# Causal mask of the attention scores: two products of 64 moving columns, one 64x64 triangle, in place of two of 128 columns

## The chip, the cores and the metric

The kernel runs on one core of one Trainium2 chip. The metric is the device time of one execution in microseconds. Before the change three runs took 2469.01, 2470.95 and 2475.01 us; the median is 2470.95.

## What is computed

One layer of a hybrid decoder block for 2048 positions and a model width of 1024, in float32: a modulated RMSNorm, a combined projection, three groups of heads side by side (mLSTM memory, forgetting attention, a chunked spatial gate), an output projection, and a feed-forward part with a causal convolution. The change lies in the attention, which has 8 heads of 64 and works on blocks of 128 queries:

```
for blk in range(s_len // Q_BLOCK):                 # Q_BLOCK = 128, s_len = 2048
    lo, hi = blk * Q_BLOCK, (blk + 1) * Q_BLOCK
    logits = (einsum('bhtd,bhsd->bhts', q[:, :, lo:hi], k[:, :, :hi]) * scale
              + F[:, :, lo:hi, None] - F[:, :, None, :hi])
    mask = (lo + arange(Q_BLOCK))[:, None] >= arange(hi)[None, :]
    logits = where(mask, logits, -inf)
    p = softmax(logits, axis=-1)
    outs.append(einsum('bhts,bhsd->bhtd', p, v[:, :, :hi]))
```

Only the last 128 keys of a query block, the diagonal block, need the mask: key column j is allowed for query row t when j <= t.

## The kernel before

The program goes through the projection, with the mLSTM and the spatial gate in between (0 to about 645 us), then the attention (to about 1010 us, its first scores beside the end of the projection), the output projection, and the feed-forward part.

In the attention, `score` (L194) makes the scores of one query block of one head against up to 1024 keys. q and k are each split into a high and a low float32r part, so a score is three products (high by high, high by low, low by high). The depth of a head is 64, half of TensorE's 128 rows. So the even key blocks of 128 lie on partitions 0 to 63 (`lower`) and the odd ones on 64 to 127 (`upper`), and each of the three terms is two matmuls, one in each row half, each moving up to four key blocks (512 columns). Both write into one PSUM pair `pr` of two banks, one bank for each half. That is line L218. `own` is the half in which the diagonal block lies; it alternates from one query block to the next.

The mask is added on TensorE as well, in L223, after the three terms and only for the chunk that holds the diagonal (`last`). There are 128 such chunks, 16 query blocks of 8 heads. Only the 64 rows of the own half can be used without touching the other half, and a mask of 128 query rows by 128 keys needs a contraction over 128. So the mask comes in two products over 64 rows each, both with 128 moving columns and a stationary matrix of 64 by 128: `identb` with `maskb` brings one half of the mask's query rows, and `idents` with `masks`, the same two with their halves swapped, brings the other. All are bf16; a masked place gets -1e30.

VectorE then runs L224 on the pair: it subtracts from the log-forget bias `nf`, writes the negated logits `L` to SBUF, and keeps their running minimum `nm`. It is also what makes the pair free for the next use; there are two pairs under the tag `pb` and one under `pc`. `weigh` takes the exponential on ScalarE (L232) and scales on GpSimd (L233, L234); `turn_pair` transposes the weights on TensorE in row halves, 64 moving columns each (L248), and copies them to SBUF (L252 to L255); `value_pair` multiplies with the values in column halves of the array (L266). The order of all these steps is a string written by hand (one letter for each: S for score, X for weigh, T, U or W for turns, V for values, Y or Z to leave), and it is kept as it stands by `tc.manual_schedule()`. So each engine has a fixed order in this stage.

The constants are made at the start of the program: on GpSimd the identity `ident` and a 128x128 triangle `m32` (L424, L425), and on VectorE the bf16 copies (L98, L103, L426, L428). After them VectorE goes on with other small constants and then waits for the first statistics of the norm (L558).

Of the kernel before, what the change touches and what calls it, by code (L numbers as in the profile page):

```python
# [10 lines left out]
BF16 = mybir.dt.bfloat16  # L11
AF = mybir.ActivationFunctionType
ALU = mybir.AluOpType
# [4 lines left out]
P = 128  # L18
# [5 lines left out]
NEG = -1.0e30  # L24
# [9 lines left out]
def trunk(  # L34
# [7 lines left out]
    V, A, G, T = nc.vector, nc.scalar, nc.gpsimd, nc.tensor  # L42
# [15 lines left out]
    cst = ctx.enter_context(tc.tile_pool(name="cst", bufs=1))  # L58
# [20 lines left out]
    ident = cst.tile([P, P], F32, name="ident")  # L79
# [14 lines left out]
    sh2 = cst.tile([P, KT], F32, name="sh2")  # L94
    cs = cst.tile([P, KT], F32, name="cs")
    gq8 = cst.tile([P, 1], F32, name="gq8")
    identb = cst.tile([P, P], BF16, name="identb")
    V.tensor_copy(identb, ident)  # L98
    maskb = cst.tile([P, P], BF16, name="maskb")
    idents = cst.tile([P, P], BF16, name="idents")  # L100
    masks = cst.tile([P, P], BF16, name="masks")
    for n in range(2):
        V.tensor_copy(idents[:, 64 * n : 64 * n + 64], ident[:, 64 - 64 * n : 128 - 64 * n])  # L103

    class Mem:

# [50 lines left out]
    def place(b):  # L157
        return 4 + b // 2 if b % 2 else 3 - b // 2
# [5 lines left out]
    def pair():  # L164
        n_pair[0] += 1
        last = three[0] and n_pair[0] % 3 == 0
        return pp.tile([P, 2, 512], F32, name="pr", tag="pc" if last else "pb")
# [26 lines left out]
    def score(h, tb, i, c):  # L194

        kk, nf = kv[h]
        q2, qs = qs_[h, tb], slice(i * P, (i + 1) * P)
        n_b = tb * 4 + i + 1
        if c == 0:
            tag = {(0, 0): "LX", (0, 1): "L2", (NH - 1, 2): "L1"}.get((h, tb), "L%d" % tb)  # L200
            L_[h, tb, i] = (
                pool.tile([P, n_b * P], F32, name="L", tag=tag),
                pool.tile([P, 2], F32, name="nm", tag="nm"), pool.tile([P, 1], F32, name="rs", tag="rs"),
            )
        L, nm, _ = L_[h, tb, i]
        n_p = min(8, n_b - 8 * c)
        ne, no = (n_p + 1) // 2, n_p // 2
        sp = pair().rearrange("p f n -> p (f n)")
        o, w = (4 - ne) * P, n_p * P
        halves_ = [  # L210
            (r, sp[:, a : a + m * P], slice(c * 512 + k0, c * 512 + k0 + m * P))
            for r, a, m, k0 in ((lower, o, ne, o), (upper, 512, no, 0)) if m
        ]
        last = c == (n_b - 1) // 8
        own = (n_b - 1) % 2
        for n, (a, b) in enumerate(((0, 0), (0, 1), (1, 0))):
            for f, (r, dst, ks) in enumerate(halves_):
                T.matmul(dst, q2[a][r, qs], kk[b][r, ks], start=n == 0, stop=n == 2 and not (last and f == own))  # L218
        if last:
            r = (lower, upper)[own]  # L220
            at = place((n_b - 1) % 8) * P
            for a, b in ((identb, maskb), (idents, masks)):
                T.matmul(sp[:, at : at + P], a[r], b[r], start=False, stop=a is idents)  # L223
        V.tensor_tensor_reduce(  # L224
            out=L[:, c * 1024 : c * 1024 + w], in0=sp[:, o : o + w], in1=nf[:, c * 1024 + o : c * 1024 + o + w],
            scale=-1.0, scalar=3.0e38 if c == 0 else nm[:, 0:1], op0=ALU.add, op1=ALU.min, accum_out=nm[:, c : c + 1],
        )
# [194 lines left out]

    m32 = pool.tile([P, P], F32, name="m32", tag="kw")
    G.memset(m32, 0.0)  # L424
    G.affine_select(m32, m32, pattern=[[-1, P]], compare_op=ALU.is_ge, fill=NEG, base=0, channel_multiplier=1)  # L425
    V.tensor_copy(maskb, m32)  # L426
    for n in range(2):
        V.tensor_copy(masks[64 * n : 64 * n + 64], m32[64 - 64 * n : 128 - 64 * n])  # L428
    V.memset(rmask, 1.0)
    V.memset(rmask.rearrange("p (n l) -> p n l", l=P)[:, :, 0:1], 0.0)  # L430

# [842 lines left out]
    for n, (half, i) in enumerate(steps):  # L1274
# [5 lines left out]
        if n == len(steps) - 1:  # L1280
            while background:
                if next(background[0], True):
                    background.pop(0)
            n_accs[0] = 2
            pool.close("proj_r")
            pp.close("proj_r")
            attention_open_right()

            load_k(0)

            def early(tb):
                for i in range(4):
                    score(0, tb, i, 0)
                    yield
                    weigh(0, tb, i)

            for tb in (1, 0):
                load_q(0, tb, "qA")
            first = [early(1), early(0)]
            load_v(0, (0, 1))  # L1300
            background += first
# [71 lines left out]
    for a in order:  # L1373
        if a == "S":
            x_ = s_list.pop(0)
            h, tb, i, c = x_
            if i == 0 and c == 0:
                n = heads.index((h, tb))
# [3 lines left out]
                if n + 1 == len(heads) or heads[n - 1][0] != h or n == 0:  # L1382
                    if h + 1 < NH and h + 1 not in kv:
                        load_k(h + 1)
                        if h % 2:
                            load_v((h + 1) // 2, range(4))
            score(*x_)
            if c == (tb * 4 + i) // 8:
                x_list.append((h, tb, i))
# [563 lines left out]
    at = lambda i, what: getattr(groups[steps[i][1], steps[i][2]], what)(steps[i][3])  # L1953
# [183 lines left out]
```

## Time and profile before

| what | value |
| --- | --- |
| median of three runs | 2470.95 us |
| profiled execution, its own time | 2468.99 us |
| its span, first to last instruction | 2467.0 us |
| granted TensorE clock, mean | 0.998 |
| TensorE products, busy | 2436.6 us (99%) |
| TensorE weight loads, busy | 1973.8 us (80%) |
| VectorE, busy | 1876.9 us (76%) |
| ScalarE, busy | 1198.9 us (49%) |
| GpSimd, busy | 378.7 us (15%) |
| attention stage | 645 to 1010 us of the span |

PE stands for TensorE's products and PEld for its weight loads, DVE for VectorE, ACT for ScalarE, POOL for GpSimd, SP for the queue that issues the DMAs. A row of a group gives line, engine, operation, tiles, shape and count, then the busy time in us, the mean duration of one in ns, and the idle time of the engine ahead of it with what ended it. A row of a timeline gives the start, the duration to the last end, engine, line, tiles, shape and the count of instructions merged in it. A row of waits gives who waited for whom, the total in us, the number of times and the longest. A row of a window gives its length, then for each engine busy time and count, then the granted clock, the share of the DMA engines and GB/s. A shape such as 64*128 64x512 is the part of the array in use (rows by columns) and the operand (partitions by elements). Matmuls are pipelined: the records of several overlap, and the busy time of a line is the time that its records cover.

### The profile page before, as it was taken

What the parts mean: (1) busy time and instruction counts of PE and PEld (TensorE: products, weight loads), DVE (VectorE), ACT (ScalarE), POOL (GpSimd) and SP (SyncE); (2) the same over time, 40 slices, a digit from 0 to 9 for tenths busy, and PEclk for the clock granted to TensorE, in tenths of its full rate; (3) what the DMA queues carried; (4) which work ended last, traced back from release to release, by engine and by line L of the source; (5) the groups of instructions that cost most, each with busy time, mean ns of one, the idle gap of its engine ahead of it and who ended that gap; (6) DMA issues with size and microseconds to landing.
All of it is one profiled execution on the core that took longest, in us unless ns stands there. A gap on an engine that the chain in (4) does not pass through costs nothing.

```text
span 2467.0 us, 39340 instructions
## 1 busy us (share of the span) xinstructions
PE 2436.6 (99%) x14553; PEld 1973.8 (80%) x14553; DVE 1876.9 (76%) x3170; ACT 1198.9 (49%) x2068; POOL 378.7 (15%) x417
## 2 busy tenths in 40 slices
PE   7999999999999999999999999999999999999999
PEld 6888888888766666788778888888888888888887
DVE  6657746476277777756798888879888878988897
ACT  5443343433367777544555444445444445444443
POOL 2023310133257665200000000000000000000000
PEclk9999999999999999999999999999999999999999
DMA  8345753545555453677332222283222229387523
GB/s 272 109 145 160 229 168 90 153 137 167 158 172 150 122 166 106 209 265 269 116 97 91 86 78 86 82 311 94 77 86 86 86 102 326 114 287 239 174 73 119
DMA packets 288823, 373.50 MB, mean 151 GB/s; under 512 B 31102, under 2 KB 181596, under 8 KB 287608
## 3 DMA queue, kind: packets, MB, share of 16 engines
q1 hardware_dynamic: 288632, 371.00, 47.6%
q8 instruction: 114, 1.87, 0.3%
q14 instruction: 77, 0.63, 0.1%
HBM read 274.34 MB, written 96.58 MB: 150 GB/s over the span
## 4 chain that ended last, share of the span: by engine, by line
PE 50%; DVE 1%; ACT 0%; issue 0%
PE ub L55 11%; PE ub L56 11%; PE ub L54 11%; PE db L56 6%; PE db L54 6%; PE db L55 6%; DVE T L1545 0%; DVE hz L1536 0%; DVE wspl L1601 0%; DVE B L1545 0%; ACT hz L1514 0%; ACT T L1541 0%; DVE s L1640 0%; DVE S L1587 0%; DVE u L1634 0%
## 5 line engine op out<-in xcount | busy, mean ns | idle before, releaser
L54 PE MATMUL acc<-wh,hh 128*128 128x512 f32 (+2 forms) x752 | 278.6, 371 | 0.0
L54 PE MATMUL ub<-T,wsph 128*128 128x512 f32 x704 | 273.9, 389 | 1.2 <-ACT wsph L1597 1.2
L55 PE MATMUL ub<-T,wsph 128*128 128x512 f32 x704 | 274.4, 390 | 0.5 <-DVE T L1545 0.5
L56 PE MATMUL ub<-T,wspl 128*128 128x512 f32 x704 | 273.9, 389 | 0.0
L56 PE MATMUL acc<-wh,hl 128*128 128x512 f32 (+2 forms) x752 | 269.6, 360 | 0.3 <-DVE hl L586 0.2
L55 PE MATMUL acc<-wl,hh 128*128 128x512 f32 (+2 forms) x752 | 268.7, 359 | 0.6 <-DVE wl L628 0.6
L55 PE MATMUL db<-wspl,wsph 128*128 128x512 f32 x616 | 239.5, 389 | 0.0
L54 PE MATMUL db<-wsph 128*128 128x512 f32 x616 | 239.5, 389 | 0.0
L56 PE MATMUL db<-wsph,wspl 128*128 128x512 f32 x616 | 239.5, 389 | 0.0
L1597 ACT CAST wsph<-S 128x512 fp32r<-128x512 f32 x176 | 109.3, 622 | 218.1 <-PE ub L55 154.4
L1740 ACT CAST wsph<-act 128x512 fp32r<-128x512 f32 x154 | 96.1, 624 | 230.1 <-PE db L55 221.5
L55 PE MATMUL ub<-B,wsph 128*128 128x512 f32 x528 | 205.6, 389 | 1.0 <-DVE B L1545 0.9
L54 PE MATMUL ub<-B,wsph 128*128 128x512 f32 x528 | 205.7, 390 | 0.0
L56 PE MATMUL ub<-B,wspl 128*128 128x512 f32 x528 | 205.4, 389 | 0.0
L224 DVE CUSTOM_DVE_ANT_0 L<-pr,nf 128x1024 f32<-128x1024 f32 (+7 forms) x128 | 124.3, 989 | 64.4 <-PE pr L218 31.1
L232 ACT ACTIVATE L<-L,nm 128x1792 f32<-128x1792 f32 (+15 forms) x128 | 153.6, 1203 | 21.3 <-DVE nm L224 18.7
L56 PEld LDWEIGHTS acc<-wh,hl 128*128 128x128 f32 x752 | 142.3, 190 | 22.1 <-DVE hl L586 0.9
L54 PEld LDWEIGHTS acc<-wh,hh 128*128 128x128 f32 x752 | 142.7, 190 | 20.9 <-issue 1.1
L55 PEld LDWEIGHTS acc<-wl,hh 128*128 128x128 f32 x752 | 142.8, 190 | 20.5 <-DVE wl L628 1.5
L55 PEld LDWEIGHTS ub<-T,wsph 128*128 128x128 f32 x704 | 132.1, 188 | 29.4 <-DVE T L1545 2.1
L54 PEld LDWEIGHTS ub<-T,wsph 128*128 128x128 f32 x704 | 132.1, 188 | 29.2 <-ACT wsph L1597 1.6
L56 PEld LDWEIGHTS ub<-T,wspl 128*128 128x128 f32 x704 | 132.1, 188 | 27.5 <-DVE wspl L1601 0.3
(331 smaller groups left out, 5497.0 us busy)
## 6 DMA issues: line engine op xcount, KB each, us to landing
w<-in_w_up_dram SPq DMA_DIRECT2D x88, 512.0 KB
wd<-in_w_down_dram SPq DMA_DIRECT2D x154, 256.0 KB
wa<-in_w_ada_dram SPq DMA_DIRECT2D x96, 256.0 KB
act_d<-yc SPq DMA_DIRECT2D x44, 512.0 KB
act<-act_d SPq DMA_DIRECT2D x44, 512.0 KB
wr<-in_w_in_dram SPq DMA_DIRECT2D x64, 256.0 KB
q<-q_d SPq DMA_DIRECT2D x128, 128.0 KB
hc_d<-hl SPq DMA_DIRECT2D x28, 512.0 KB
```

The costliest lines, as they stand in the source:

```text
L54: T.matmul(ps, lh, rh, start=start, stop=False, skip_group_check=resume)
L55: T.matmul(ps, lh, rl, start=False, stop=False, skip_group_check=resume)
L56: T.matmul(ps, ll, rh, start=False, stop=stop, skip_group_check=resume)
L224: V.tensor_tensor_reduce(out=L[:, c * 1024 : c * 1024 + w], in0=sp[:, o : o + w], in1=nf[:, c * 1024 + o : c * 1024 + o + w], scale=-1.0, ...
L232: A.activation(L, L, AF.Exp, bias=nm[:, n : n + 1], scale=-1.0, accum_out=rs)
L1597: A.copy(self.wa[p][0], self.source(p))
L1740: A.copy(hi, v)
```

## The change

The diagonal block is cut in four quarters of 64 by 64. Upper left and lower right need the same triangle; upper right (queries 0 to 63, keys 64 to 127) is masked wholly, and lower left not at all. The new `tri` is that triangle, 64x64, once on each row half: row i holds -1e30 at columns j >= i. `sel_a` and `sel_b` are stationary matrices of 64 by 128 that choose a row of it for each query. `sel_a` gives query t (0 to 62) the row t + 1, which masks j > t, and nothing to the queries from 63 on; its product goes to the first 64 key columns. `sel_b` gives queries 64 to 126 the same rows in turn, and queries 0 to 63 row 0, which is masked in all columns; its product goes to the last 64. The two products still have 64 rows and 128 stationary columns each, but 64 moving columns in place of 128. The constants are made in another way; `affine_select` on GpSimd has another base and is otherwise the same.

```
-    identb = cst.tile([P, P], BF16, name="identb")
-    V.tensor_copy(identb, ident)
-    maskb = cst.tile([P, P], BF16, name="maskb")
-    idents = cst.tile([P, P], BF16, name="idents")
-    masks = cst.tile([P, P], BF16, name="masks")
-    for n in range(2):
-        V.tensor_copy(idents[:, 64 * n : 64 * n + 64], ident[:, 64 - 64 * n : 128 - 64 * n])
+    tri = cst.tile([P, 64], BF16, name="tri")
+    sel_a, sel_b = (cst.tile([P, P], BF16, name=n) for n in ("sel_a", "sel_b"))
+    V.memset(sel_a, 0.0)
+    V.memset(sel_b, 0.0)
+    for r in (0, 64):
+        V.tensor_copy(sel_a[r : r + 64, 0:63], ident[r : r + 64, r + 1 : r + 64])
+        V.tensor_copy(sel_b[r : r + 64, 64:127], ident[r : r + 64, r + 1 : r + 64])
+        V.memset(sel_b[r : r + 1, 0:64], 1.0)
...
-            for a, b in ((identb, maskb), (idents, masks)):
-                T.matmul(sp[:, at : at + P], a[r], b[r], start=False, stop=a is idents)
+            for a, o_ in ((sel_a, 0), (sel_b, 64)):
+                T.matmul(sp[:, at + o_ : at + o_ + 64], a[r], tri[r], start=False, stop=a is sel_b)
...
-    G.affine_select(m32, m32, pattern=[[-1, P]], compare_op=ALU.is_ge, fill=NEG, base=0, channel_multiplier=1)
-    V.tensor_copy(maskb, m32)
-    for n in range(2):
-        V.tensor_copy(masks[64 * n : 64 * n + 64], m32[64 - 64 * n : 128 - 64 * n])
+    G.affine_select(m32, m32, pattern=[[-1, P]], compare_op=ALU.is_ge, fill=NEG, base=-1, channel_multiplier=1)
+    for r in (0, 64):
+        V.tensor_copy(tri[r : r + 64], m32[r : r + 64, r : r + 64])
```

On TensorE the order of instructions is the same at all 128 places. This is one of them in the attention, before: the last of a score's six products, the mask (loads and products, stationary tile last), then two scores' products of the next query block and its mask.

```order
L218 MATMUL pr<-kk,q 128x256
L223 LDWEIGHTS identb
L223 MATMUL pr<-maskb,identb 128x128
L223 LDWEIGHTS idents
L223 MATMUL pr<-masks,idents 128x128
L218 MATMUL pr<-kk,q 128x512 x6
L218 MATMUL pr<-kk,q 128x384 x6
L223 LDWEIGHTS identb
```

The same place in the changed kernel, where the lines have moved down by one:

```order
L219 MATMUL pr<-kk,q 128x256
L224 LDWEIGHTS sel_a
L224 MATMUL pr<-tri,sel_a 128x64
L224 LDWEIGHTS sel_b
L224 MATMUL pr<-tri,sel_b 128x64
L219 MATMUL pr<-kk,q 128x512 x6
L219 MATMUL pr<-kk,q 128x384 x6
L224 LDWEIGHTS sel_a
```

Nothing has moved there: the operands differ, and the products write 64 columns each. ScalarE, GpSimd and the DMA queue have the same instructions in the same order too.

On VectorE the start of the program differs. The rows from the third small constant on, with a minus before and a plus now:

```order
-L415 MEMSET fc 36x1
-L421 MEMSET R 128x512
-L98 CAST identb<-ident 128x128
-L103 CAST idents<-ident 128x64 x2
-L426 CAST maskb<-m_182 128x128
-L428 CAST masks<-m_182 64x128 x2
+L99 MEMSET sel_a 128x64
+L100 MEMSET sel_b 128x64
+L416 MEMSET fc 36x1
+L422 MEMSET R 128x512
+L104 MEMSET sel_b 1x64 x2
+L102 CAST sel_a<-ident 64x63
```

Three more casts of 64x63 and the two of `tri` follow (`m_182` is `m32`); six casts have become six smaller ones and four memsets. Everything behind them on VectorE stands in the same order as before.

## The prediction

> **What bounds the kernel now.** I read the totals first, then the four stages in windows, and then stayed in the one stage that the change touches. The page gives the span and the busiest engine:
>
> ```profile
> span 2467.0 us, 39340 instructions
> PE 2436.6 (99%) x14553; PEld 1973.8 (80%) x14553; DVE 1876.9 (76%) x3170; ACT 1198.9 (49%) x2068; POOL 378.7 (15%) x417
> ```
>
> The profiled execution took 2468.99 us, 2.0 us more than its span; the median of the runs shown is 2470.95 us, another 2.0 above it. So I make the sum against 2469.0 and carry the difference over to 2470.95. About 0.3% (7.4 us) is what a measurement of this kernel can tell from no change: the three runs alone lie 6 us apart.
>
> The mask products are all in the attention stage, 645 to 1010 us. First the whole stage in windows (busy us of each engine, with the count of instructions), then the same window for the mask line L223 alone, then the longest waits of the stage that involve it:
>
> ```profile
> 645.00:1010.00 365.00, 363.76 (x4260) 249.51 (x4258) 259.98 (x490) 257.48 (x390) 220.27 (x256) 1.00 0.50 141
> ```
>
> ```profile
> 645.00:1010.00 365.00, 36.19 (x256) 14.35 (x256) 1.00 0.50 141
> ```
>
> ```profile
> DVE L L224 <- PE pr L223: 37.7, 50, 3.2
> ACT L L232 <- DVE nm L224: 18.7, 14, 4.9
> PEld pr L218 <- DVE nm L224: 18.6, 27, 0.8
> PEld pr L248 <- DVE nm L224: 10.2, 14, 0.8
> ```
>
> TensorE is busy for 363.8 of 365 us, VectorE for 260, ScalarE for 257, at a granted clock of 1.00. So TensorE sets this stage. VectorE waits for the mask 50 times, 37.7 us in all, and in turn the weight loads wait 41 times (18.6 + 10.2 us) until VectorE has emptied a PSUM pair: two engines in a loop, with TensorE the tighter one. The mask line is busy for 36.2 us over 256 products. That number is a trap, since it counts the latency of products that overlap others; what a product takes from the row half it runs in has to be read from starts.
>
> The instructions of that line (ns, least, median, greatest), and one place where the pair runs between two scores:
>
> ```profile
> L223 PEld LDWEIGHTS <-identb x128: 92/93/97, 648.6 to 1000.6; 64*128 64x128 bf16 x128
> L223 PE MATMUL pr<-maskb,identb x128: 226/227/231, 648.6 to 1000.7; 64*128 64x128 bf16 x128
> L223 PEld LDWEIGHTS <-idents x128: 95/97/99, 648.6 to 1000.7; 64*128 64x128 bf16 x128
> L223 PE MATMUL pr<-masks,idents x128: 216/216/216, 648.7 to 1000.7; 64*128 64x128 bf16 x128
> ```
>
> ```profile
> 700.60 0.09 PEld L223 LDWEIGHTS <-identb 64*128 64x128 bf16 x1
> 700.60 0.23 PE L223 MATMUL pr<-maskb,identb 64*128 64x128 bf16 x1
> 700.61 0.10 PEld L223 LDWEIGHTS <-idents 64*128 64x128 bf16 x1
> 700.67 0.22 PE L223 MATMUL pr<-masks,idents 64*128 64x128 bf16 x1
> 700.67 0.53 PEld L218 LDWEIGHTS pr<-kk,q 64*128 64x128 f32 x5
> ```
>
> The second product starts 0.07 us after the first, though each has a duration of 0.22: some 0.16 us of every record is the way through the array. By the ends the pair is tighter: the first lasts 11 ns longer than the second (227 against 216), so the ends are 0.07 less 0.011, about 0.06, apart.
>
> **How much a column costs.** Scores of different width, and the transposes, which also move 64 columns in one row half:
>
> ```profile
> L218 PE MATMUL pr<-kk,q 64*128 64x512 f32 x528 | 91.0, 412 | 0.9 <-ACT vt L792 0.7 <-DVE nm L224 0.2
> L218 PE MATMUL pr<-kk,q 64*128 64x384 f32 x192 | 35.7, 353 | 0.2 <-DVE nm L224 0.2
> L248 PEld LDWEIGHTS pr<-ident,L x2142: 134/139/142, 686.5 to 1009.9; 64*128 64x128 f32 x195
> L248 PE MATMUL pr<-ident,L x2142: 213/222/275, 686.7 to 1010.0; 64*128 64x64 f32 x195
> ```
>
> 128 columns less shorten a score from 412 to 353 ns, 59 ns. That agrees with the 0.06 between the two mask products: they stream 128 columns each in about 0.06 us, and 64 columns should take 0.03.
>
> **The first product (64 instead of 128 columns).** It saves 0.03 us if the second product's weights are there in time. The nearest row for that is the run of 16 transposes, which alternate between the two row halves, eight in each:
>
> ```profile
> 703.93 0.68 PEld L248 LDWEIGHTS pr<-ident,L 64*128 64x128 f32 x16
> 704.10 0.66 PE L248 MATMUL pr<-ident,L 64*128 64x64 f32 x16
> ```
>
> Less one latency of 0.22 the eight take 0.44 us, or 0.063 us from one to the next in a half: twice what their 64 columns would stream in. So a load of 128 float32 columns can set the pace of a 64-column product, and if the bf16 load did the same, nothing would be saved. But its record is 97 ns against 139, 42 ns shorter; 63 less 42 is 21 ns, below the 30 of the stream. I therefore take 0.03, with 0 as the other end. The Trainium skill bears on this in "TensorE: Matmul & The Clock Gate", section "LDWEIGHTS (loading the stationary operand)": a load's time goes by its columns, 128 in both versions, not by its rows, at 107 ns for 128. By that alone the two mask products would stand 107 ns apart; the trace has about 60, so the figure doesn't hold for these bf16 loads.
>
> **The second product.** Its own 0.03 us is hidden wherever what follows waits for a float32 load anyway. In the order of instructions 89 of the 128 pairs are followed by a score (L218), 19 by a transpose (L248), 14 by a value product (L266) and 6 by a product of the output projection. Three score loads in each of the two halves, beside products of 128 columns:
>
> ```profile
> 700.23 0.86 PE L218 MATMUL pr<-kk,q 64*128 64x128 f32 x7
> 700.20 0.42 PEld L218 LDWEIGHTS pr<-kk,q 64*128 64x128 f32 x6
> L218 PEld LDWEIGHTS pr<-kk,q x1104: 182/185/193, 646.1 to 1000.5; 64*128 64x128 f32 x184
> ```
>
> Less one record of 0.185 that is 0.235 us for two steps, 0.12 each, where 128 columns stream in 0.06. The next score's load starts with the second product (both at 700.67), and 0.12 covers 0.06 as well as 0.03. The transposes' 0.063 does the same. So nothing is saved for 108 pairs. The other 20 are followed by an instruction in another shape of the array:
>
> ```profile
> 705.08 0.22 PE L223 MATMUL pr<-masks,idents 64*128 64x128 bf16 x1
> 705.22 0.20 PEld L266 LDWEIGHTS op<-pT,vv 128*64 128x64 f32 x4
> 705.23 0.65 PE L266 MATMUL op<-pT,vv 128*64 128x256 f32 x4
> ```
>
> It starts 0.15 us after the mask: it waits for the rows to run dry, so that a shorter second product counts there, 20 x 0.03 = 0.6 us.
>
> **The sum for TensorE.** 128 x 0.03 = 3.8 us of the row half that owns the diagonal. That half is the later one of its score (it has as many key blocks as the other or one more, and the mask), so the saving is on the path when the next thing needs both halves. But the owner alternates from one query block to the next (`own`): where two scores of opposite owners follow without such a meeting in between, the two savings lie side by side and count once. That bounds the term between 1.9 and 3.8 us; I take 2.6, nearer to the lower end since S often follows S in the order written by hand. With 0.6 for the 20, 3.2 us.
>
> **VectorE.** The last product ends 0.03 + 0.03 us earlier, and 50 waits end with it: at most 3.0 us less idle time there. TensorE is the tighter engine, so I count none of it beyond the 3.2; if the loop ran through VectorE at each mask, the whole would be 128 x 0.06 = 7.7 us, the upper end of the gain. ACT, POOL and SP have the same instructions in the same order.
>
> **The start.** VectorE makes the constants in the first microseconds:
>
> ```profile
> 1.59 0.21 DVE L98 CAST identb<-ident 128x128 bf16<-128x128 f32 x1
> 1.73 0.28 DVE L103 CAST idents<-ident 128x64 bf16<-128x64 f32 x2
> 1.93 0.21 DVE L426 CAST maskb<-m 128x128 bf16<-128x128 f32 x1
> 2.16 0.46 DVE L428 CAST masks<-m 64x128 bf16<-64x128 f32 x2
> 4.35 0.06 DVE L445 MEMSET mcar<- 4x1 f32 x1
> 6.27 0.16 DVE L558 TENSOR_TENSOR st<-st 128x1 f32<-128x1 f32 x1 [1.78 <-ACT jk L554]
> ```
>
> Six casts (1.16 us) go; four small memsets of 0.06 to 0.1 and six casts of about 64x64, at most 0.23 each (half of 0.46), come: 0.3 + 1.4 = 1.7, so up to 0.5 us more. VectorE then idles 1.78 us for ScalarE before L558, which hides it; without that cover it would be 0.5 us.
>
> **Forecast:** 2469.0 - 3.2 = 2465.8 against the profiled execution, 2470.95 - 3.2 = **2467.8 us** against the median. Chance 0.55.
>
> **Rivals.** (1) The weight load sets the pace. Then the second product still starts 0.06 us after the first, both shortenings are hidden, and only the 20 drains (0.6 us) and the earlier end of the last product remain: about 2470.3. For it speak the transposes' 0.063; against it the shorter bf16 load. Chance 0.25. The skill has a rule for it on the same page, section "Back-to-back issue gap": in a stream of load and product the spacing is set by both, some 81 ns for 128 columns, far from halved by fewer columns. The 60 ns here is below that figure, so this case's rows bear it out for the float32 loads and not for the mask.
>
> (2) Every pair gives its full 0.06 us, through the loop with VectorE: 7.7 us, 2463.3. For it speak the 50 waits for the mask, against it TensorE's 363.8 of 365 us. Chance 0.12.
>
> (3) The line's busy time halves: 36.2 / 2 = 18.1 us, 2452.9. Against it, transposes with 64 columns last 222 ns and mask products with 128 last 216: the records hardly shrink. Chance 0.04.
>
> (4) Slower: the pair now writes two separate column ranges of the bank, with two partial weights, and if the array ran dry between the two, as it does ahead of L266, the second would start 0.15 instead of 0.06 us after the first. That is 0.09 x 128 = 11.5 us, 2482.5; from 0.03 more per pair it would decide against the saving. Against it, 64-column transposes into changing places of a bank follow each other at 0.063. Chance 0.04.
>
> **Range and chances.** 2463 to 2473 takes in rivals 1 and 2 with the forecast, and 2 us above no change for the scatter of a median. Faster by over 0.3% (below 2463.5) is rival 3 and half of rival 2: 0.10. Slower by over 0.3%: 0.04. The rest, 0.86, is within 0.3%.
>
> **What would show it.** In the changed profile the second mask product starts about 0.03 to 0.04 us after the first (0.06: rival 1; 0.15: rival 4), with loads as before at 92 to 97 ns. The records last about 0.03 us less (190 to 200 ns). The next score still starts its load with the second product. The attention stage ends 2 to 4 us earlier, and L558's first wait on VectorE stays above 1 us. The forecast is wrong if the pair is closer together and the stage still ends when it did, or if the stage gains over 6 us.

## The result and the profile after

The changed kernel took 2484.67 us (median of 5 runs, 2483.56 to 2487.43) against 2470.95 before: slower by 13.7 us, a ratio of 1.0057 (95% interval 1.0046 to 1.0068). The forecast was 2467.8, and the range ended at 2473.

The page of the changed kernel begins so:

```profile
span 2482.7 us, 39344 instructions
PE 2450.6 (99%) x14553; PEld 1973.8 (80%) x14553; DVE 1878.2 (76%) x3174; ACT 1199.4 (48%) x2068; POOL 378.4 (15%) x417
```

The span is 15.7 us longer, TensorE's busy time 14.0 us. The first place to look is the mask itself, now line L224: its four instructions, and one pair in the order of time.

```profile
L224 PEld LDWEIGHTS <-sel_a x128: 92/93/96, 650.3 to 999.9; 64*128 64x128 bf16 x128
L224 PE MATMUL pr<-tri,sel_a x128: 199/200/203, 650.3 to 999.9; 64*128 64x64 bf16 x128
L224 PEld LDWEIGHTS <-sel_b x128: 95/97/99, 650.3 to 999.9; 64*128 64x128 bf16 x128
L224 PE MATMUL pr<-tri,sel_b x128: 190/190/191, 650.3 to 999.9; 64*128 64x64 bf16 x128
```

```profile
701.86 0.09 PEld L224 LDWEIGHTS <-sel_a 64*128 64x128 bf16 x1
701.86 0.20 PE L224 MATMUL pr<-tri,sel_a 64*128 64x64 bf16 x1
...
701.87 0.10 PEld L224 LDWEIGHTS <-sel_b 64*128 64x128 bf16 x1
701.90 0.19 PE L224 MATMUL pr<-tri,sel_b 64*128 64x64 bf16 x1
```

The second product starts 0.04 us after the first, where it was 0.07, and the records are 26 ns shorter (216 to 190). The mask does what was forecast. So does the stage around it, from the first score to the start of the last value product. The rows are those of the score and value lines, before and then after; the two times behind the durations are the first and the last start.

```profile
L218 PE MATMUL pr<-kk,q x1104: 217/386/501, 646.1 to 1000.7; 64*128 64x512 f32 x92, 64*128 64x384 f32 x33, 64*128 64x256 f32 x33, 64*128 64x128 f32 x26
...
L266 PE MATMUL op<-pT,vv x640: 272/592/644, 690.3 to 1015.3; 128*64 128x512 f32 x128, 128*64 128x256 f32 x32
```

```profile
L219 PE MATMUL pr<-kk,q x1104: 215/386/502, 647.8 to 999.9; 64*128 64x512 f32 x91, 64*128 64x384 f32 x34, 64*128 64x256 f32 x33, 64*128 64x128 f32 x26
...
L267 PE MATMUL op<-pT,vv x640: 272/592/644, 691.6 to 1014.5; 128*64 128x512 f32 x128, 128*64 128x256 f32 x32
```

646.1 to 1015.3 is 369.2 us; 647.8 to 1014.5 is 366.7. The attention gains 2.5 us, and at its end the changed kernel is 0.8 us ahead. All of the loss lies behind it, where no line of the program differs. There the same stretch, 1210 to 2080 us (most of the up projection and the first 15 to 30 us of the down projection), holds fewer products; before, then after:

```profile
1210.00:2080.00 870.00, 867.33 (x3819) 715.57 (x3818) 745.14 (x996) 426.43 (x707) 0.00 (x0) 1.00 0.35 117
```

```profile
1210.00:2080.00 870.00, 867.50 (x3771) 704.20 (x3770) 734.13 (x978) 419.35 (x694) 0.17 (x1) 1.00 0.34 112
```

TensorE is as full as before (867 of 870 us) at a clock of 1.00, and gets through 3771 products in place of 3819: 230.7 ns each instead of 227.8. It waits no longer; the products are slower. The groups of the up projection (`ub`) and of the down projection (`db`), before:

```profile
L54 PE MATMUL ub<-T,wsph 128*128 128x512 f32 x704 | 273.9, 389 | 1.2 <-ACT wsph L1597 1.2
...
L56 PE MATMUL ub<-B,wspl 128*128 128x512 f32 x528 | 205.4, 389 | 0.0
...
L54 PE MATMUL db<-wsph 128*128 128x512 f32 x616 | 239.5, 389 | 0.0
```

and after:

```profile
L54 PE MATMUL ub<-T,wsph 128*128 128x512 f32 x704 | 277.0, 394 | 1.2 <-ACT wsph L1597 1.2
...
L56 PE MATMUL ub<-B,wspl 128*128 128x512 f32 x528 | 206.7, 391 | 0.0
...
L54 PE MATMUL db<-wsph 128*128 128x512 f32 x616 | 239.5, 389 | 0.0
```

`ub<-T` takes 394 ns each instead of 389, `ub<-B` 391 instead of 389, `db` is as it was. That was the clue: T and B are made of seven groups of tiles, three of four T groups and one of three B groups lie in pools on the left side of SBUF, and everything that `db` reads lies on the right.

The left pools stand on top of the constants (`cst`). The change took 1024 bytes per partition from the constants and put 640 in their place. So every left tile moved down by 384 bytes, and the right ones stayed. From the starts of the products in the two traces and the addresses that the two programs give their tiles, the mean time from one 512-column product to the next:

| products, operands | distance, before | ns | distance, after | ns |
| --- | --- | --- | --- | --- |
| ub, moving T1, T4 (left), weights right | 0 | 226.7 | 128 | 233.0 |
| ub, moving T3, B22 (left), weights right | 0 | 226.9 | 128 | 232.9 |
| ub, moving B11, B21 (right), weights right | 0 | 226.8 | 0 | 227.6 |
| ub, moving T2 (right), weights right | 0 | 226.8 | 0 | 228.1 |
| db, both right | 0 | 226.7 | 0 | 226.7 |
| projection, both left | 0 | 228.3 | 0 | 228.2 |

"Distance" is the address of the moving operand less that of the weights loaded beside it, modulo 256 bytes. 2112 products of `ub` with 6.1 ns more make 12.9 us, and the 1584 beside them with 0.8 to 1.3 ns more 1.5; no run shows why these, at distance 0 in both, grew at all. In the output projection about half of 768 products (the ones with one operand on each side) go the same way, 2.3 us. Together 16.7, less the 2.5 gained in the attention: 14.2 of the 15.7 us by which the spans of these two executions differ; the medians lie 13.7 apart. The other 1.5 are there before the attention starts (646.1 and 647.8 us); the traces of the first experiments below start it at 647.7 to 648.9, the one with the old mask too, so that this is no effect of the new mask.

### The profile page after: what moved, and what is told of

It is laid out like the page before. It is cut to its first block, busy times and chain, and to the rows that moved or that the text cites. A ratio compares the mean times of both kernels' runs of the same rounds, so it can differ in the third digit from the quotient of the medians.

```text
span 2482.7 us, 39344 instructions
## 1 busy us (share of the span) xinstructions
PE 2450.6 (99%) x14553; PEld 1973.8 (80%) x14553; DVE 1878.2 (76%) x3174; ACT 1199.4 (48%) x2068; POOL 378.4 (15%) x417
## 4 chain that ended last, share of the span: by engine, by line
PE 50%; DVE 1%; ACT 0%; issue 0%
PE ub L55 11%; PE ub L56 11%; PE ub L54 11%; PE db L54 6%; PE db L55 6%; PE db L56 6%; DVE T L1545 0%; DVE hz L1536 0%; DVE wspl L1601 0%; DVE B L1545 0%; ACT hz L1514 0%; ACT T L1541 0%; DVE s L1640 0%; DVE S L1587 0%; DVE u L1634 0%
## 5 line engine op out<-in xcount | busy, mean ns | idle before, releaser
L54 PE MATMUL ub<-T,wsph 128*128 128x512 f32 x704 | 277.0, 394 | 1.2 <-ACT wsph L1597 1.2
L55 PE MATMUL ub<-T,wsph 128*128 128x512 f32 x704 | 277.4, 394 | 0.4 <-DVE T L1545 0.2
L56 PEld LDWEIGHTS ub<-T,wspl 128*128 128x128 f32 x704 | 132.1, 188 | 30.9 <-DVE wspl L1601 0.2
```

What stands on the lines that cost most here:

```text
L54: T.matmul(ps, lh, rh, start=start, stop=False, skip_group_check=resume)
L55: T.matmul(ps, lh, rl, start=False, stop=False, skip_group_check=resume)
L56: T.matmul(ps, ll, rh, start=False, stop=stop, skip_group_check=resume)
```

## The experiments

Three theories stood. A: the distance between the moving operand and the weights loaded beside it, modulo 256 bytes, sets the pace of a full float32r product. B: the absolute address of the left tiles does. C: the new mask products or constants slow the later stages in some other way.

**The left tiles back where they were.** The changed kernel with an unused tile among the constants:

```
+    pad = cst.tile([P, 96], F32, name="pad")
```

> The changed kernel with an unused tile of 384 bytes per partition among the constants, so that every tile on the left side of SBUF has the address that it had before the change; the computation is that of the changed kernel. Theory A (a full 128-row product takes about 6 ns longer when its moving operand and the weights loaded beside it lie 128 bytes apart modulo 256; the change took 384 bytes from the constants and so moved the left tiles against the right ones): the 15.6 us of the up projection and output projection are gone, the mask's own saving of about 2.5 us stays, 2468 us (2466 to 2470). Theory B (the absolute address of the left tiles decides): the same here, 2468. Theory C (the new mask products or the new constants make the later stages slow, whatever the addresses): 2484 as the changed kernel.

2469.08 us against 2470.93 of the kernel before beside it, ratio 0.9991 (0.9982 to 0.9999). The up projection in this run:

```profile
L54 PE MATMUL ub<-T,wsph 128*128 128x512 f32 x704 | 273.9, 389 | 1.2 <-ACT wsph L1599 1.2
...
L56 PE MATMUL ub<-B,wspl 128*128 128x512 f32 x528 | 205.5, 389 | 0.0
```

The loss is gone to the tenth of a microsecond, with the new mask in place. C falls. What is left is the mask alone: 1.9 us faster, with an interval of 0.2 to 4.4.

**The right tiles moved instead.**

```
+    pad_r = tc.alloc_tile_pool(name="pad_r", bufs=1, side="right")
+    pad_r.tile([P, 96], F32, name="pad")
```

> The changed kernel with an unused tile of 384 bytes at the right end of SBUF, so that the right tiles move by as much as the left ones did: left tiles stay where the changed kernel has them, distances are those of before. Theory A (distance modulo 256): 2468 us (2466 to 2470), up products whose moving operand is on the left back at 227 ns from start to start. Theory B (absolute address of the left tiles): 2484, and products with a moving operand on the left at 233. Theory C (mask products or constants themselves): 2484.

2469.47 us, ratio 0.9993 (0.9984 to 1.0002), and the products at 389 ns again:

```profile
L54 PE MATMUL ub<-T,wsph 128*128 128x512 f32 x704 | 273.9, 389 | 1.2 <-ACT wsph L1600 1.2
```

Here the left tiles lie where the slow kernel has them, and the products are fast. B falls; it is the distance.

**The shift without the change.** The kernel before, with both old identities cut from one tile:

```
-    identb = cst.tile([P, P], BF16, name="identb")
-    V.tensor_copy(identb, ident)
...
-    idents = cst.tile([P, P], BF16, name="idents")
...
+    identx = cst.tile([P, 192], BF16, name="identx")
+    V.tensor_copy(identx[:, 0:P], ident)
+    V.tensor_copy(identx[:, P:192], ident[:, 0:64])
+    identb, idents = identx[:, 0:P], identx[:, 64:192]
```

> The kernel before, with its old mask products of 128 columns, but the two identities kept in one tile of 192 columns, which takes 128 bytes from the constants and moves the left tiles by 128 against the right ones. Theory A: the slow distances without the change, 2470.95 + 15.6 = 2486.5 us (2484 to 2489). Theory B: another absolute address, 128 off instead of 384: as A or unchanged at 2471. Theory C: 2471, since neither the new products nor the new constants are there.

2487.34 us, ratio 1.0061 (1.0047 to 1.0074), 0.8 us beyond the number expected:

```profile
span 2485.6 us, 39339 instructions
...
L54 PE MATMUL ub<-T,wsph 128*128 128x512 f32 x704 | 277.0, 394 | 1.2 <-ACT wsph L1596 1.2
...
L56 PE MATMUL ub<-B,wspl 128*128 128x512 f32 x528 | 206.7, 391 | 0.0
```

The same rows as in the changed kernel, with the old mask. 128 bytes fewer among the constants are enough for the whole loss. The attention stage, measured as above, lasts 369.4 us in this trace and 369.2 before, so the shift costs nothing there; with the new mask it lasts 366.6 to 368.1 us in four traces.

**Another good distance.** The changed kernel with a tile of 128 bytes:

```
+    pad = cst.tile([P, 32], F32, name="pad")
```

> The changed kernel with an unused tile of 128 bytes, so that the left tiles lie 256 bytes from where they were before. Theory A with a period of 256 bytes: 2468 us (2466 to 2470). With a period of 512 bytes, or if only the very distances of before are good: over 2480. Theory C: 2484.

2469.01 us, ratio 0.9990 (0.9982 to 0.9999). The period of 256 bytes holds. Both versions with padded constants beat the kernel before by about 1.9 us, at the edge of what can be told.

**TensorE by itself.** A loop of products, run once, with the moving operand shifted by `off` bytes (`o` is the same in elements):

```
T.matmul(pt, w[:, 128 * (n % 8) : 128 * (n % 8) + 128],
         m[:, 512 * (n % 4) + o : 512 * (n % 4) + o + 512],
         start=n == 0, stop=n == N - 1)
```

> A kernel of its own that computes nothing of the reference: TensorE alone, 256 products of 128x128 by 128x512 in float32r for each distance between the moving operand and the weights (0, 0 again, 16, 32, 64, 96, 128, 160, 192, 224, 256, 384, 512, 640 bytes), then the same in bf16 for 0, 32, 64, 96, 128, 192, 256, 384, then a stretch in which the weights stand alternately at distance 0 and 128. The other engines do nothing beside it. Theory A (a read of the moving operand and a load of weights disturb each other on TensorE's side, by their distance modulo 256): 227 ns from one product to the next at 0, 256 and 512, about 233 at 128, 384 and 640, something between at the others; the alternating stretch about 230. If the writes and reads of the other engines take part (theory D), all distances take 227 here. For bf16, whose loads are shorter, A expects less than half the loss.

The number in a tile's name is the distance in bytes, r stands for float32r and b for bf16; then busy us for 256 products, and mean ns of one:

```profile
L68 PE MATMUL r160x<-mv,wt 128*128 128x512 f32 x256 | 60.1, 396 | 0.0
L68 PE MATMUL r32x<-mv,wt 128*128 128x512 f32 x256 | 59.9, 395 | 0.0
...
L68 PE MATMUL r128x<-mv,wt 128*128 128x512 f32 x256 | 59.9, 395 | 0.0
...
L68 PE MATMUL r384x<-mv,wt 128*128 128x512 f32 x256 | 59.9, 395 | 0.0
...
L68 PE MATMUL r64x<-mv,wt 128*128 128x512 f32 x256 | 58.8, 391 | 0.0
L68 PE MATMUL r256x<-mv,wt 128*128 128x512 f32 x256 | 58.2, 389 | 0.0
L68 PE MATMUL r512x<-mv,wt 128*128 128x512 f32 x256 | 58.2, 389 | 0.0
L68 PE MATMUL b0x<-mb,wb 128*128 128x512 bf16 x256 | 55.4, 379 | 0.0
L68 PE MATMUL b128x<-mb,wb 128*128 128x512 bf16 x256 | 55.4, 379 | 0.0
```

389 against 395 ns, as in the kernel, with nothing running on the other engines: D, by which these would have to take part, falls too. Of the distances tried only 0, 256 and 512 are free of the loss (226.7 ns from start to start, at 0 once the first products are over). I had expected something between at the odd distances; 64 is in between (391), and 16, 32, 96, 160, 192 and 224 are about as slow as 128 (394 to 396). In bf16 no distance makes a difference. The alternating stretch gave 234 and 231 ns by its starts (leaving out its first step), which decides nothing.

**Which weights.** The same loop, again run once, with moving operands and weights alternating between two places so that a product's own weights and the next product's lie at different distances:

> TensorE alone again, computing nothing of the reference: 256 float32r products for each pattern. Moving operands and weights alternate between two places 128 bytes apart, so that a product's own weights and the weights loaded beside it (the next product's) can be set at different distances from its moving operand: good (both at 0), own (its own at 128, the next at 0), next (its own at 0, the next at 128), bad (both at 128); each with 512 and with 256 moving columns. Theory A1 (the read of the moving operand meets the load of the next weights): own as good, 227 ns; next as bad, 233 ns. Theory A2 (it is the product's own weights): the other way round. If the loss is one of the load, it is the same 6 ns per product with 256 columns (about 120 ns from product to product); if it goes with the stream, about 3 ns.

In the names x stands for 512 columns; the last two rows have 256.

```profile
L67 PE MATMUL badx<-mv,wt 128*128 128x512 f32 x256 | 59.6, 395 | 0.0
L67 PE MATMUL ownx<-mv,wt 128*128 128x512 f32 x256 | 59.0, 392 | 0.0
L67 PE MATMUL nextx<-mv,wt 128*128 128x512 f32 x256 | 58.6, 390 | 0.0
...
L67 PE MATMUL goodx<-mv,wt 128*128 128x512 f32 x256 | 58.2, 389 | 0.0
L67 PE MATMUL goody<-mv,wt 128*128 128x256 f32 x256 | 30.9, 283 | 0.0
L67 PE MATMUL bady<-mv,wt 128*128 128x256 f32 x256 | 30.5, 281 | 0.0
```

Neither A1 nor A2: from 58.2 us the distance of the own weights adds 0.8, that of the next ones 0.4, both together 1.4. With 256 columns the bad distance costs nothing (30.5 against 30.9 us, 119 and 120 ns from start to start). These shares don't explain the alternating stretch above: there every product has one of its two distances bad, which here gives 228 or 230 ns, and it took 231 to 234. Why the distance matters to TensorE stays open.

**What the mask is worth.** First a kernel that leaves out the mask (good distances, no products of L224):

> The changed kernel with the good distances (384 bytes of padding), and the causal mask left out altogether: no L224 products and no loads for them. It bounds what the mask can cost. If TensorE's row half carries the pair on its path, the new pair takes about 0.06 to 0.10 us between two scores, 8 to 13 us in all: 2456 to 2461. If what follows the pair waits for other things anyway (VectorE emptying the pairs, the float32 loads), less than 4 us: 2465 to 2469.

2458.95 us, ratio 0.9945 (0.9930 to 0.9960). The page:

```profile
span 2456.7 us, 38832 instructions
```

0.55% is 13.6 us (interval 9.9 to 17.3), or 106 ns for each of 128 old pairs. The new pair cost 1.9 us less in the first experiment, so about 91 ns. The traces give less: without the mask the attention stage lasts 357.6 us, against 369.2 with the old pair (91 ns for each) and 366.6 to 368.1 with the new (70 to 82). By either measure the pair is on the path of TensorE, as the prediction had it. Then the pair three times in a row, new and old:

```
-            for a, o_ in ((sel_a, 0), (sel_b, 64)):
-                T.matmul(sp[:, at + o_ : at + o_ + 64], a[r], tri[r], start=False, stop=a is sel_b)
+            for m in range(3):
+                for a, o_ in ((sel_a, 0), (sel_b, 64)):
+                    T.matmul(sp[:, at + o_ : at + o_ + 64], a[r], tri[r], start=False, stop=m == 2 and a is sel_b)
```

> The changed kernel with the good distances, and the new pair of mask products issued three times in a row (the mask is added three times). Two more pairs of 2 x 0.029 us for 128 chunks: 256 x 0.058 = 14.8 us if all on the path, 2483.8; half of it (2476) where the owners of two scores lie side by side.

> The kernel before with the old pair of mask products issued three times in a row. Two more pairs of 2 x 0.056 us for 128 chunks: 256 x 0.112 = 28.7 us if all on the path, 2499.6; half of it 2485. Against the run with three new pairs it should be 14 to 18 us slower if streaming sets the pace of the pair, and within 4 us of it if the loads of the weights, which are the same in both, set it.

2484.40 us, ratio 1.0048 (1.0032 to 1.0064), and 2498.10, ratio 1.0105 (1.0087 to 1.0124). The records of the second products, new and old:

```profile
L227 PE MATMUL pr<-tri,sel_b x384: 190/190/191, 650.1 to 1014.6; 64*128 64x64 bf16 x192
```

```profile
L224 PE MATMUL pr<-masks,idents x384: 216/216/216, 649.4 to 1027.5; 64*128 64x128 bf16 x192
```

Two more old pairs cost 1.05% or 25.9 us, 101 ns a pair (112 forecast); two more new ones 1.0048 less 0.9991, 14.1 us, 55 ns a pair (58 forecast). The two runs lie 13.7 us apart, a little under the 14 to 18 expected if the streams set the pace and far from the 4 for the loads. Starts inside such a row, old and then new:

```profile
700.37 0.22 PE L224 MATMUL pr<-maskb,identb 64*128 64x128 bf16 x1
700.43 0.22 PE L224 MATMUL pr<-masks,idents 64*128 64x128 bf16 x1
...
700.48 0.22 PE L224 MATMUL pr<-maskb,identb 64*128 64x128 bf16 x1
```

```profile
702.83 0.19 PE L227 MATMUL pr<-tri,sel_b 64*128 64x64 bf16 x1
...
702.86 0.19 PE L227 MATMUL pr<-tri,sel_a 64*128 64x64 bf16 x1
...
702.89 0.19 PE L227 MATMUL pr<-tri,sel_b 64*128 64x64 bf16 x1
```

The median from one product to the next is 56 ns with 128 columns and 29 with 64, with a weight load of 128 columns each time. So the streams set the pace of a pair, 46 ns less with half the columns, and the rival of the weight loads is wrong.

In the kernel the single pair saves only 1.9 us / 128 = 15 ns of these 46. What comes behind the pair shows where part of the rest goes. In the traces of before and after, the next product on TensorE starts a median of 28 and 29 ns after the second mask product where it is a score, 53 and 29 ns where it is a transpose, and 146 and 120 ns where it has another shape. One of the last kind after the change (the prediction shows one of before):

```profile
706.27 0.19 PE L224 MATMUL pr<-tri,sel_b 64*128 64x64 bf16 x1
...
706.39 0.65 PE L267 MATMUL op<-pT,vv 128*64 128x256 f32 x4
```

Ahead of a score, then, the shorter second product gains nothing. That the float32 load is the reason, as the prediction had it, no run takes apart.

## Why the prediction was wrong

The step that failed is the bound of the whole sum. "The mask products are all in the attention stage" and "ACT, POOL and SP have the same instructions in the same order" closed the search for side effects. So the sum, 2469.0 - 3.2, carries every other stage over unchanged: a term put at nothing for no other reason than the order of the instructions. The text compared instructions, operands and order, and never asked where the tiles lie. The four constants of 1024 bytes became three of 640, which stands in the diff, and the left pools moved with them. By the traces the term is 16.5 us: from the last value product to the first of the up projection 185.2 us in place of 182.7, and the up projection 865.0 in place of 851.0. With the distances restored, the kernel takes 15.6 us less (2469.08 against 2484.67), six times what the attention gained. No rival had it. Rival 4 ended near the measured time (2482.5) by another mechanism, which the trace refutes: the second product comes after 0.04 us, not 0.15. Its number is a coincidence.

The term of the mask, point by point:

- The first product's 0.03 us: right. The starts went from 0.07 to 0.04 us, and extra pairs cost 55 ns where 58 was expected.
- The second product hidden: right ahead of the scores, where the next product starts 28 and 29 ns after it. The float32 load as the reason is not shown. Ahead of the transposes, where the text saved nothing, the next product came 24 ns earlier.
- The 20 places with another shape: 26 ns each, 0.5 us of the 0.6 counted. The six that the text gives to the output projection are products of the first projection (`acc`).
- The sum of 3.2 us for TensorE: 1.9 measured at equal distances (interval 0.2 to 4.4 us). The text's bounds, 1.9 to 3.8 and 0.6 on top, give 2.5 to 4.4, so it was rather too high. The attention stage gained 2.5 us in the changed kernel's trace, within the forecast 2 to 4.
- Rival 1, the weight load: refuted by the starts, 0.04 us apart where it asked for 0.06, and by the three pairs in a row.
- Rivals 2 and 3, a gain of 7.7 and 18.1 us: outside the interval of 0.2 to 4.4. VectorE's waits for the mask, which rival 2 would have shortened, are no shorter in the changed kernel's trace: 40.4 us in 46 waits, against 37.7 in 50 before.
- The start: VectorE's idle time before L558 went from 1.78 to 1.28 us, the 0.5 us that were counted, hidden as foreseen:

```profile
6.21 0.16 DVE L558 TENSOR_TENSOR st<-st 128x1 f32<-128x1 f32 x1 [1.28 <-ACT jk L554]
```

Could it have been seen? Not the price: in the trace of before all full products of the up projection lay at distance 0, and nothing showed another. But the exposure was there, as 2112 products of 227 ns on a TensorE 99% busy with an operand on each side of SBUF. The Trainium skill bears on it in "SBUF — State Buffer", section "Who interferes with whom": TensorE has two independent read ports, for the moving operand and for the weights, and never waits on anyone. By that alone the distance would make no difference. The bf16 runs here agree with it (379 ns at every distance); the float32r runs do not (389 against 395 ns with TensorE alone).

## What to carry to other kernels

A change in the size of any tile moves what is stacked on it. Before calling an edit local, ask which operands change their distance to which others, and see in the profile whether groups that the edit doesn't touch kept their mean duration. In float32r, with full rows and 512 moving columns, keep the moving operand and the weights a multiple of 256 bytes apart; an unused tile of 128 or 384 bytes did that here and was worth 15 us.

## What the runs showed that was not expected

- A float32r product of 128 rows and 512 columns takes 227 ns at a distance of 0, 256 or 512 bytes between moving operand and weights, and 232 to 234 at 16 to 224 (229 at 64), 384 and 640. In bf16 it takes 216 ns at every distance tried. At 256 columns distances of 0 and 128 cost the same (117 to 120 ns).
- A pair of bf16 products with 64 rows and 64 columns, each with its own load of 128 columns, costs 55 ns in a row of such pairs; with 128 columns 101 ns.
